# Moving ten of a sample's 32 expert dot-product steps from the output projection to the last dense blocks, in quarters of 512 columns

## The chip, the cores and the metric

The kernel runs on one core of one Trainium2 chip. The metric is device time in microseconds (us), the median of the runs shown. The engines are PE (matrix multiply), DVE (vector), ACT (scalar), POOL (GpSimd, which also issues the gathers) and SP (which here only issues transfers). Each engine executes its own queue strictly in order, and engines wait for one another through semaphores.

## The reference

One decoder layer over 256 prompt tokens and 32 sample tokens (8 sequences of 4): an input projection, an RWKV group and an attention group, one output projection, a layer norm, and then a mixture of 16384 single-row experts. The part that matters here is that last one:

```python
q = (xt @ wq).reshape(n, P_HEADS, 2, P_DKEY // 2)
...
expert = jnp.take_along_axis(cand_e, tpos, axis=-1)
gate = jax.nn.softmax(tv, axis=-1).astype(x.dtype)
...
h = jax.nn.gelu(jnp.einsum('cd,chkd->chk', xb, u_tab[eb]), approximate=False)
return jnp.einsum('chk,chkd->cd', gb * h, v_tab[eb])
```

Every token has 8 heads with 16 chosen experts each, so 128 dot products of its 2048-wide row with rows of `u_tab`. All arrays are float32.

## The kernel before

**Prompt tokens.** The 256 prompt tokens are two tiles of 128 partitions. Their dot products are split by columns. Columns 0 to 895 (`UG`) are done by gathering: for each tile and each of 128 expert slots, `gather` (L453, POOL) fetches one 896-wide row for each partition into a buffer of the ring `rows` (`NRW` = 5 buffers), and one DVE instruction (L1825) multiplies it with the token's row and sums it. There are 256 such dots. The other nine groups of 128 columns (`NDB`) are done densely: for each of 128 blocks `dense(i1)` loads a 576 KB tile `ur` on SP (L1896, `NUR` = 5 buffers), runs 18 matmul instructions on PE (L1899) into one of five PSUM banks `ph`, and copies the result with ACT (L1900) to `AW`. The loop over `i1` spreads the dots that are left evenly over the 128 blocks. In its first 80 blocks DVE also chooses the experts of the second prompt tile (`choose_parts`), and at `i1 == 80` it computes that tile's gates (`gates(1)`, L1454 to L1458, with an exponential on ACT). `table(0)` (L1836 to L1841) follows at block 90.

**The sample.** The 32 sample tokens take all 128 partitions: four groups of heads by 32 tokens, with 32 slots each. So there are 32 *steps*, and each step is a 2048-wide dot product for each partition. `sample_dots` does a step in two halves of 1024 columns: a gather of 512 KB from `uh2` (the table seen as half rows; `GI[2]` and `IG` hold the indices of the first and second halves), and a DVE instruction (L1586) whose sum goes to one column of `hd`. `hd` is a view of a small tile, `shT`, that is no longer needed. The 32 steps run in two places:

- Steps 0 to 13 (`NSD` = 14) at the end of `sample_chain`, in the ring `cw` (`NCW` = 5). The first stands in the attention's weave; the rest are woven with the second half of the output projection: `weave((chain, NSD), (out_part(8, YN), 16, 400))`. The last number gives `out_part` a higher priority in the scheduler.
- Steps 14 to 31, called `late`, in the ring `sr`: six (`NLD`) around the first layer norm, then two for each head of the query projection, all done before the dense blocks.

`sample_formed` then adds the two halves (L1591), applies the Gelu on ACT and multiplies by the gates. Its result is first needed in the stage after the dense blocks (`weigh`).

**The output projection.** `out_part(8, YN)` is 16 pieces of work. A piece loads 512 KB of `w_out` (L1682), makes a rounded copy `wh` on ACT (L1684) and the remainder `wl` on DVE, every fourth on POOL (L1685), each with two buffers, and runs 12 matmuls of 512 columns (L1690). After every four pieces DVE adds the two sums into `x` (L1698) and takes statistics of it (L1699). The layer norm follows.

**What sets the order.** A scheduler with a timeline simulation orders each engine's queue when the kernel is built: by program order as priority, unless something is not ready or its ring has no free buffer. `issue_after` holds instructions behind a named one. After the dense blocks, `pick` (L1933) is the first work of the stage `weigh`.

Of the kernel before, what the change touches and what calls it, by code (L numbers as in the profile page):

```python
# [10 lines left out]
F32 = mybir.dt.float32  # L11
F32R = mybir.dt.float32r
I32 = mybir.dt.int32
U32 = mybir.dt.uint32
AF = mybir.ActivationFunctionType
OP = mybir.AluOpType
AX = mybir.AxisListType
PSUM = bass.MemoryType.PSUM
P = 128

D = 2048
NT = 288
NPR = 256
# [9 lines left out]
WS = 100  # L33
CPOOL = 0
NSO = 4
NSD = 14
NLD = 6
PRI = 200
WB = 4
# [12 lines left out]
NCB = 10  # L52
# [96 lines left out]
def hybrid_decode_step(ctx: ExitStack, tc: tile.TileContext, a, outs, dbg=None):  # L149
# [203 lines left out]
            gp.dma_start(shA[26 * b:26 * b + 26, hf, :],  # L353
                         a["state_shift"][0, 4 * hf + b, 0, :3328].rearrange("(c p) -> c p", p=P))
    shT = cp([P, 2, 4, 26], "shT")
    hd = shT.rearrange("p h b c -> p (h b c)")[:, :64].rearrange("p (q s) -> p q s", q=2)
    def split_x(pb, k_, t_):
        sc.copy(XH0[:, k_, t_], pb)
        ve.tensor_tensor(XL0[:, k_, t_], pb, XH0[:, k_, t_].bitcast(F32), OP.subtract)
# [1052 lines left out]

    def choose_parts(h, pool, S, TV):

        HV, HI, HF = (pool([P, 2, 16], nm, ty) for nm, ty in (("HVb", F32), ("HIb", U32), ("HFb", F32)))
        for c in range(2):
            top16(S[:, c, :], HV[:, c, :], HI[:, c, :])
            yield 1
        for c in range(2):
            ve.tensor_scalar(HF[:, c], HI[:, c], 1.0 if c else 1.0 * P, 0.0, op0=OP.mult, op1=OP.add)  # L1420
        CV, CE = (pool([P, NCAND], nm) for nm in ("CVb", "CEb"))
        for dst, src in ((CV, HV), (CE, HF)):
            o = 0
            for i0, ni, w in CAND:
                ve.tensor_tensor(dst[:, o:o + ni * w].rearrange("p (i j) -> p i j", i=ni),
                                 src[:, 0, i0:i0 + ni, None].to_broadcast([P, ni, w]),
                                 src[:, 1, None, :w].to_broadcast([P, ni, w]), OP.add)
                o += ni * w
        yield 1
        TI, TF = (pool([P, 16], nm, ty) for nm, ty in (("TIb", U32), ("TFb", F32)))  # L1430
        top16(CV, TV[:, h, :], TI)
        ve.tensor_copy(TF, TI)
        yield 1
        hit = rp([P, UG], "rows", bufs=NRW)[:, :16 * NCAND].rearrange("p (a b) -> p a b", a=16)
        ve.tensor_tensor(hit, iota[:, None, :NCAND].to_broadcast([P, 16, NCAND]),
                         TF[:, :, None].to_broadcast([P, 16, NCAND]), OP.is_equal)
        ve.tensor_tensor(hit, hit, CE[:, None, :].to_broadcast([P, 16, NCAND]), OP.mult)
        yield 1
        EF = pool([P, 16], "EFb")
        ve.tensor_reduce(EF, hit, AX.X, OP.add)  # L1440
        sc.copy(GI[1][:, 16 * h:16 * h + 16], EF)
        yield 1
# [44 lines left out]

    w_out, w_q = a["w_out"][0], a["peer_wq"][0]
    utab, vtab = a["peer_u"][0], a["peer_v"][0]
    uh2 = utab.rearrange("n (q c) -> (n q) c", q=2)  # L1490
    iota = C0("iota")

# [87 lines left out]
    def sample_dots(ring, x4, n0, n1):  # L1580

        for s_ in range(n0, n1):
            for q in range(2):
                r_, x_, h_ = ring(), x4[:, 1024 * q:1024 * q + 1024], hd[:, q, s_:s_ + 1]
                gather(r_, uh2, (IG if q else GI[2])[:, s_:s_ + 1])
                ve.scalar_tensor_tensor(r_, r_, 1.0, x_, op0=OP.mult, op1=OP.mult, accum_out=h_)  # L1586
            yield 1

    def sample_formed():

        ve.tensor_tensor(hd[:, 0], hd[:, 0], hd[:, 1], OP.add)  # L1591
        sc.activation(hd[:, 0], hd[:, 0], AF.Gelu)
        ve.tensor_tensor(GE[2], hd[:, 0], GE[2], OP.mult)

# [175 lines left out]
    sx4 = sq_([P, D], "sx4")  # L1770
    for g in range(4):
        sy.dma_start(sx4[32 * g:32 * g + 32, :], X1D[NPR:NT, :])
    late = sample_dots(lambda: sq_([P, 1024], "sr", bufs=5), sx4, NSD, 32)
    with tc.issue_after(normed.ins):
        for _ in take(late, NLD):
            pass
# [53 lines left out]
    def table(t):  # L1830

        pb = bank("pb")
        for q, (op_, v_) in enumerate(((OP.logical_shift_right, 7), (OP.bitwise_and, 127))):
            ii = up([P, P], "ii", I32, bufs=2)
            iff = ii.bitcast(F32)
            ve.tensor_scalar(ii, GI[t], v_, None, op0=op_)  # L1836
            ve.tensor_copy(iff, ii)
            pe.transpose(pb[:, 128 * q:128 * q + 128], iff, ident)
        pe.transpose(pb[:, 256:384], GE[t], ident)
        pe.transpose(pb[:, 384:], HD[t], ident)  # L1840
        sc.copy(TB[:, :, P * t:P * t + P], pb.rearrange("p (a b) -> p a b", a=4))  # L1841
# [34 lines left out]
    with tc.issue_after(chosen.ins), tc.issue_after(last_.ins):  # L1876
        for _ in late:
            pass
        sample_formed()
    sq_.close()  # L1880
    kw_.close()
    for q in range(0, NDB, 3):
# [20 lines left out]
    for i1 in range(P):  # L1903
        mm, end = dense(i1)
        n_ = early + -(-(2 * P - early) * (i1 + 1) // P)
        dot(n_ - got[1])
        with tc.issue_after(last_dot[0].ins):
            for _ in take(later, 6 * (i1 + 1) // NCB - 6 * i1 // NCB):
                pass
            if i1 == 8 * NCB:  # L1910
                for _ in later:
                    pass
                gates(1, up, TV[1])
        if i1 == 8 * NCB + 10:
            with tc.issue_after(mm.ins), tc.issue_after(end.ins):
                table(0)
# [276 lines left out]
```

## Time and profile before

| | |
|---|---|
| median of 3 runs | 2458.02 us (2453.15 to 2464.91) |
| the profiled execution | 2450.29 us, of which 2448.5 us is the span |
| PE, DVE, ACT, POOL busy | 92%, 72%, 34%, 54% of the span |
| moved by the DMA engines | 684.07 MB, 279 GB/s on average |
| second half of the output projection, first matmul to last | 995.33 to 1059.42 us |
| dense blocks on PE, first matmul to last | 1202.3 to 1700 us |
| last dot of the prompt | ends at 1702.2 us |

The table's places are in us from the start of the span. Busy time is an average over stages with different limits, so what matters is which wait ends last in each of the two stages that the change touches: the output projection at about 1000 us, and the last third of the dense blocks, from about 1520 to 1700 us.

### The profile page before, as it was taken

The numbers are of one execution on the slowest core, as the hardware profiler recorded it, in microseconds if no ns is written. First come the engines' busy times: TensorE is split into PE (matmuls) and PEld (weight loads), VectorE is DVE, ScalarE is ACT, GpSimd is POOL, SyncE is SP. The second block draws the span as 40 slices with busy tenths as digits, with TensorE's granted clock in tenths as the row PEclk, the third lists the DMA queues.
The fourth block names the chain that finished last, engine by engine and source line by source line (L and its number), as shares of the span: only waits on it lengthen the run. The fifth ranks groups of instructions, "written<-read, shape, count | busy, mean of one in ns | idle before, by whom it ended". The sixth has DMA issues, their size and how long they took to land.

```text
span 2448.5 us, 42558 instructions
## 1 busy us (share of the span) xinstructions
PE 2255.8 (92%) x15628; PEld 1888.4 (77%) x15628; DVE 1762.0 (72%) x4049; ACT 823.4 (34%) x1601; POOL 1332.6 (54%) x1347
## 2 busy tenths in 40 slices
PE   7988999897988998679999999999999899999996
PEld 7877889894645565558888888887777788887885
DVE  4788766555563355687877777556777899998888
ACT  4433222223432334221111111111777544444343
POOL 5687522324355011666766556565443688886772
PEclk9989999998896799789999999999999999999998
DMA  7777885448578784979999999999664799999994
GB/s 219 215 232 233 257 236 172 131 135 250 200 248 250 249 274 172 317 253 348 317 367 377 391 371 387 345 395 345 186 188 142 284 362 360 358 367 356 345 360 183
DMA packets 327600, 684.07 MB, mean 279 GB/s; under 512 B 82270, under 2 KB 200992, under 8 KB 326464
## 3 DMA queue, kind: packets, MB, share of 16 engines
q1 hardware_dynamic: 246176, 342.58, 42.2%
q0 software_dynamic: 81216, 338.78, 38.6%
q8 instruction: 123, 2.02, 0.3%
q14 instruction: 85, 0.70, 0.1%
HBM read 665.69 MB, written 23.88 MB: 282 GB/s over the span
## 4 chain that ended last, share of the span: by engine, by line
PE 29%; DMA 9%; DVE 8%; issue 7%; POOL 4%; ACT 1%; POOLq 0%; DVEq 0%; SPq 0%; ACTq 0%
PE pb L2107 20%; DMA rows<-in_peer_u_g,gi 8%; POOL rows L453 4%; PE px L1945 3%; DVE rows L1825 2%; PE pa L1978 2%; PE pj L1855 2%; PE pt L1937 1%; PE fs L1997 1%; DVE sr L1586 1%; DVE vl L2100 1%; DMA wraw<-in_peer_wq 0%; ACT vh L2099 0%; PE pa L1690 0%; DVE cw L1586 0%
## 5 line engine op out<-in xcount | busy, mean ns | idle before, releaser
L1899 PE MATMUL ph<-Xfd,ur 128*128 128x256 f32 x2304 | 497.6, 379 | 0.0
L1899 PEld LDWEIGHTS ph<-Xfd,ur 128*128 128x128 f32 x2304 | 437.6, 190 | 59.4
L453 POOL DMA_INDIRECT rq<-in_peer_v_g,gi x256 | 382.2, 1493 | 145.8 <-DVE fP L2080 85.6
L453 POOL DMA_INDIRECT rows<-in_peer_u_g,gi x256 | 313.3, 1224 | 189.3 <-DVE rows L1825 119.0
L1825 DVE SCALAR_TENSOR_TENSOR rows<-rows,x1a 128x896 f32<-128x896 f32 x256 | 278.8, 1097 | 136.2 <-DMA rows<-in_peer_u_g,gi 135.5
L422 PE MATMUL pj<-XH,wl 128*128 128x288 f32 (+1 forms) x752 | 233.5, 311 | 15.8 <-DVE wl L417 9.1
L422 PE MATMUL pj<-XH,wh 128*128 128x288 f32 (+1 forms) x752 | 232.1, 309 | 14.6 <-DVE ss L752 6.0
L422 PE MATMUL pj<-XL,wh 128*128 128x288 f32 (+1 forms) x752 | 228.0, 303 | 0.0
L2080 DVE SCALAR_TENSOR_TENSOR fP<-rq,ge,fP 128x640 f32<-128x640 f32 x254 | 223.7, 881 | 2.5
L2107 PE MATMUL pb<-vl,ah 128*128 128x512 f32 (+1 forms) x768 | 205.9, 376 | 0.8
L2107 PE MATMUL pb<-vh,al 128*128 128x512 f32 (+1 forms) x768 | 205.0, 375 | 0.0
L1900 ACT COPY AW<-ph 128x256 f32<-128x256 f32 x128 | 76.6, 612 | 370.5 <-PE ph L1899 362.7
L2107 PE MATMUL pb<-vh,ah 128*128 128x512 f32 (+1 forms) x768 | 185.6, 376 | 13.4 <-ACT vh L2099 10.9
L415 ACT CAST wh<-wraw 128x512 fp32r<-128x512 f32 (+1 forms) x188 | 115.1, 616 | 240.3 <-PE pj L422 191.1
L2107 PEld LDWEIGHTS pb<-vh,ah 128*128 128x128 f32 x768 | 144.1, 194 | 35.5 <-ACT vh L2099 13.9
L422 PEld LDWEIGHTS pj<-XH,wl 128*128 128x128 f32 (+1 forms) x752 | 145.8, 194 | 26.8 <-DVE wl L417 12.4
L476 DVE SCALAR_TENSOR_TENSOR CA<-co,wbc,CA 128x256 f32<-128x256 f32 x248 | 131.5, 568 | 46.5 <-DMA co<-in_cache_cmp_kv,gidx 46.5
L422 PEld LDWEIGHTS pj<-XH,wh 128*128 128x128 f32 (+1 forms) x752 | 146.1, 194 | 21.0 <-ACT wh L415 6.7
L2107 PEld LDWEIGHTS pb<-vl,ah 128*128 128x128 f32 x768 | 144.1, 194 | 22.7 <-DVE vl L2100 3.8
L2107 PEld LDWEIGHTS pb<-vh,al 128*128 128x128 f32 x768 | 144.5, 194 | 19.3
L422 PEld LDWEIGHTS pj<-XL,wh 128*128 128x128 f32 (+1 forms) x752 | 146.4, 195 | 1.5 <-issue 1.2
L417 DVE TENSOR_TENSOR wl<-wraw,wh 128x512 fp32r<-128x512 f32 (+1 forms) x141 | 100.8, 722 | 49.0 <-ACT wh L415 48.7
(871 smaller groups left out, 4335.6 us busy)
## 6 DMA issues: line engine op xcount, KB each, us to landing
ur<-in_peer_u_t SPq DMA_DIRECT2D x128, 576.0 KB
wraw<-in_w_in SPq DMA_DIRECT2D x152, 256.0 KB
cw<-in_w_out SPq DMA_DIRECT2D x32, 512.0 KB
wraw<-in_w_out SPq DMA_DIRECT2D x32, 512.0 KB
wraw<-in_peer_wq SPq DMA_DIRECT2D x32, 512.0 KB
cw<-in_peer_wq SPq DMA_DIRECT2D x32, 512.0 KB
wraw<-in_w_in SPq DMA_DIRECT2D x64, 128.0 KB
co<-in_state_win_kv SPq DMA_DIRECT2D x16, 512.0 KB
```

The source lines that it names most:

```text
L415: sc.copy(wh[:, :, :n], w[:, :, :n])
L417: i_ = en.tensor_tensor(wl[:, :, :n], w[:, :, :n], wh[:, :, :n].bitcast(F32), OP.subtract)
L422: last[2] = pe.matmul(pb[:n, :nt], wi[:, k, :n], xi[(o + k) // 8][:, (o + k) % 8, :nt], start=(o + k == 0 and wi is wh and xi is xh), stop ...
L453: gp.indirect_dma_start(out=dst, out_offset=None, in_=rows_, in_offset=bass.IndirectOffsetOnAxis(ap=ix, axis=0))
L476: ve.scalar_tensor_tensor(d_, x_, w_, d_, op0=OP.mult, op1=OP.add)
L1825: i_ = ve.scalar_tensor_tensor(r_, r_, 1.0, X1a[t], op0=OP.mult, op1=OP.mult, accum_out=h_)
L1855: pe.matmul(pb[:, :NPR], w[:, k, :], XT[:, o + k, :], start=(o + k == 0), stop=(o + k == 15))
L1899: mm = pe.matmul(ph[:, :NPR], w[:, e, :], Xfd[:, e, :], start=(e == 0), stop=(e == NDB - 1))
L1900: return mm, sc.copy(AW[:, i1 // 64, :, i1 % 64], ph[:, :NPR])
L1945: pin(pe.matmul(px[:, 128 * e:128 * e + 128].rearrange("p (c j) -> p c j", c=2), oT[:, e, :], AW[:, :, 4 * u + e, :], start=True, stop=True))
L2080: ve.scalar_tensor_tensor(fP[t], r_, w_, fP[t], op0=OP.mult, op1=OP.add)
L2107: pe.matmul(acc[3 * t + q][:, :n_], wi[:, P * t:P * t + P], xi[:, 512 * q:512 * q + n_], start=(k == 0 and wi is ah and xi is vh), stop=(k ...
```

## The change

Of the sample's 32 steps, only four (0 to 3) stay at the end of `sample_chain`; `late` now holds steps 4 to 21, again 18 steps; and steps 22 to 31 (`NSU` = 10) go into the loop over the dense blocks, one each at blocks 82, 86, ..., 118. There a step is four quarters of 512 columns, each with a gather of 256 KB from `uq4` into a buffer of the ring `rows`, shared with the prompt's dots, and a DVE instruction with a sum of its own. For them the sample's rows are loaded again on SP (four transfers, at block 80) into the place of the scores `S1`, and four small DVE instructions compute the indices after the gates. `sample_formed` moves behind the last of these steps. Besides, `choose_parts` now uses the tiles that `choose` used before it instead of its own, and `table` has a third buffer `ii`.

```diff
-NSD = 14
+NSD = 4
+NSU = 10
...
-    hd = shT.rearrange("p h b c -> p (h b c)")[:, :64].rearrange("p (q s) -> p q s", q=2)
+    sh_ = shT.rearrange("p h b c -> p (h b c)")
+    hd = sh_[:, :64].rearrange("p (q s) -> p q s", q=2)
+    hx, ix = (t_[:, 64 + 4 * NSU * n:64 + 4 * NSU * (n + 1)].rearrange("p (s q) -> p s q", q=4)
+              for n, t_ in enumerate((sh_, sh_.bitcast(I32))))
...
-        HV, HI, HF = (pool([P, 2, 16], nm, ty) for nm, ty in (("HVb", F32), ("HIb", U32), ("HFb", F32)))
+        HV, HI, HF = (pool([P, 2, 16], nm, ty) for nm, ty in (("HV", F32), ("HI", U32), ("HF", F32)))
...
+    uq4 = utab.rearrange("n (q c) -> (n q) c", q=4)
...
-        ve.tensor_tensor(hd[:, 0], hd[:, 0], hd[:, 1], OP.add)
+        ve.tensor_tensor(hd[:, 0, :32 - NSU], hd[:, 0, :32 - NSU], hd[:, 1, :32 - NSU], OP.add)
+        ve.tensor_reduce(hd[:, 0, 32 - NSU:], hx, AX.X, OP.add)
         sc.activation(hd[:, 0], hd[:, 0], AF.Gelu)
...
-    late = sample_dots(lambda: sq_([P, 1024], "sr", bufs=5), sx4, NSD, 32)
+    late = sample_dots(lambda: sq_([P, 1024], "sr", bufs=5), sx4, NSD, 32 - NSU)
...
-            ii = up([P, P], "ii", I32, bufs=2)
+            ii = up([P, P], "ii", I32, bufs=3)
...
-        sample_formed()
...
                 gates(1, up, TV[1])
+                for q in range(4):
+                    ve.tensor_scalar(ix[:, :, q], GI[2][:, 32 - NSU:], 2.0, float(q), op0=OP.mult, op1=OP.add)
+        if i1 == 8 * NCB:
+            x4 = dp([P, 8, 2 * P], "S1").rearrange("p a b -> p (a b)")
+            for g in range(4):
+                sy.dma_start(x4[32 * g:32 * g + 32, :], X1D[NPR:NT, :])
+        if i1 > 8 * NCB and i1 % 4 == 2 and i1 // 4 - 2 * NCB < NSU:
+            k = i1 // 4 - 2 * NCB
+            with tc.issue_after(last_dot[0].ins):
+                for q in range(4):
+                    r_ = rp([P, UG], "rows", bufs=NRW)[:, :512]
+                    gather(r_, uq4, ix[:, k, q:q + 1])
+                    ve.scalar_tensor_tensor(r_, r_, 1.0, x4[:, 512 * q:512 * q + 512], op0=OP.mult, op1=OP.mult,
+                                            accum_out=hx[:, k, q:q + 1])
+                if k == NSU - 1:
+                    sample_formed()
```

More of the change, by code (lines that the diff above doesn't have):

```diff
@@ L1420, in choose_parts @@
             ve.tensor_scalar(HF[:, c], HI[:, c], 1.0 if c else 1.0 * P, 0.0, op0=OP.mult, op1=OP.add)
-        CV, CE = (pool([P, NCAND], nm) for nm in ("CVb", "CEb"))
+        CV, CE = (pool([P, NCAND], nm) for nm in ("CV", "CE"))
         for dst, src in ((CV, HV), (CE, HF)):
@@ L1429, in choose_parts @@
         yield 1
-        TI, TF = (pool([P, 16], nm, ty) for nm, ty in (("TIb", U32), ("TFb", F32)))
+        TI, TF = (pool([P, 16], nm, ty) for nm, ty in (("TI", U32), ("TF", F32)))
         top16(CV, TV[:, h, :], TI)
@@ L1438, in choose_parts @@
         yield 1
-        EF = pool([P, 16], "EFb")
+        EF = pool([P, 16], "EF", bufs=2)
         ve.tensor_reduce(EF, hit, AX.X, OP.add)
```

## Prediction

> **What bounds the kernel now.** I read the page's head and its chain of waits first, to see which stages the end hangs on; then the busy time in stretches of 10 us in the two stages touched; then, in each, who waited for whom, the groups, and each engine's order of time.
>
> The page:
>
> ```profile
> span 2448.5 us, 42558 instructions
> PE 29%; DMA 9%; DVE 8%; issue 7%; POOL 4%; ACT 1%; POOLq 0%; DVEq 0%; SPq 0%; ACTq 0%
> PE pb L2107 20%; DMA rows<-in_peer_u_g,gi 8%; POOL rows L453 4%; PE px L1945 3%; DVE rows L1825 2%; PE pa L1978 2%; PE pj L1855 2%; PE pt L1937 1%; PE fs L1997 1%; DVE sr L1586 1%; DVE vl L2100 1%; DMA wraw<-in_peer_wq 0%; ACT vh L2099 0%; PE pa L1690 0%; DVE cw L1586 0%
> ```
>
> The prompt's gathers (rows: transfer, POOL, DVE) are the second largest part of the chain, after the last stage's matmuls. The steps that leave the projection (cw L1586) round to 0%, but the shares only add to some 58%: the chain is lost before the projection is over, so its stage has to be read from its own waits.
>
> The end of the dense blocks. Three stretches of 10 us (busy PE, PEld, DVE, ACT, POOL, then granted clock, DMA share, GB/s), the third for comparison with the first two:
>
> ```profile
> 1540.00:1550.00 10.00, 10.00 (x48) 8.79 (x48) 0.00 (x0) 2.94 (x5) 1.65 (x2) 1.00 0.90 332
> 1550.00:1560.00 10.00, 10.00 (x50) 8.82 (x49) 6.69 (x18) 2.15 (x5) 4.20 (x4) 1.00 0.71 242
> 1650.00:1660.00 10.00, 10.00 (x48) 8.81 (x47) 6.13 (x11) 1.49 (x3) 5.73 (x6) 1.00 1.02 409
> ```
>
> The transfers of 1570 to 1690 us and the gathers issued in them:
>
> ```profile
> DMA packets 9505, 47.43 MB, mean 395 GB/s; under 512 B 1519, under 2 KB 1519, under 8 KB 9497
> rows<-in_peer_u_g,gi POOLq DMA_INDIRECT x64, 7.6
> ```
>
> The groups of 1551 to 1703 us (busy, mean ns, idle time before and what ended it), then the gathers and the dots of that window by tile, with the landing times:
>
> ```profile
> L453 POOL DMA_INDIRECT rows<-in_peer_u_g,gi x77 | 95.8, 1244 | 59.5 <-DVE rows L1825 45.6 <-issue 12.7 <-ACT AW L1900 1.2
> L1825 DVE SCALAR_TENSOR_TENSOR rows<-rows,x1a 128x896 f32<-128x896 f32 x82 | 89.0, 1093 | 58.1 <-DMA rows<-in_peer_u_g,gi 58.0
> ```
>
> ```profile
> L453 POOL DMA_INDIRECT rows<-in_peer_u_g,gi x77: 951/957/1872, 1552.6 to 1695.5; - x77
> L1825 DVE DVE_READ_ACCUMULATOR rows<-rows,x1a x82: 77/83/85, 1552.3 to 1702.2; 128x1 f32 x82
> DMA to landing us min/median/max: 5.0/7.5/8.3
> ```
>
> The tile `ur` (first and last start), and DVE in order of time:
>
> ```profile
> L1899 PE MATMUL ph<-Xfd,ur x2304: 379/379/382, 1202.3 to 1699.8; 128*128 128x256 f32 x192
> L1896 SPq DMA_DIRECT2D ur<-in_peer_u_t x128: 327/328/1104, 1180.0 to 1680.8; - x128
> ```
>
> ```profile
> 1550.50 0.29 DVE L1456 TENSOR_REDUCE sm<-ge 128x8 f32<-128x128 f32 x1 [11.69 <-ACT ge L1455]
> 1556.11 0.36 DVE L1836 TENSOR_SCALAR ii<-gi 128x128 int32<-128x128 int32 x2 [2.74 <-PE pb L1838]
> ```
>
> PE is full and never waits for `ur`: (1699.8-1202.3)/128 = 3.89 us a block. The dots end at 1702.2, 2.4 us behind PE, so two things end this stage together. The dots are not held by an engine: DVE is idle 58 us of the 151 from 1551 to 1702, always for a transfer, and POOL waits 45.6 us for a buffer that DVE frees. They are held by transfers: from 1570 to 1690 (the 47.43 MB row) the DMA engines move 395 GB/s at a share of about 1.0, and 64 gathers are issued, one per 120/64 = 1.88 us. The only slack is 1540 to 1560, where DVE stood 11.69 us for the gates' exponential and then 2.74 us for `table(0)`.
>
> The projection, in two stretches, then its waits and groups of 975 to 1062 us:
>
> ```profile
> 1010.00:1020.00 10.00, 10.00 (x34) 7.92 (x34) 4.97 (x8) 2.65 (x3) 4.34 (x4) 0.73 1.03 402
> 1050.00:1060.00 10.00, 8.43 (x36) 6.28 (x35) 9.97 (x13) 1.90 (x2) 3.14 (x1) 1.00 0.74 264
> ```
>
> ```profile
> PE pa L1690 <- DVE wl L1685: 11.5, 6, 5.9
> PE pb L727 <- DVE O L721: 5.6, 1, 5.6
> PE pa L1690 <- POOL wl L1685: 1.7, 2, 1.5
> ```
>
> ```profile
> L1586 DVE SCALAR_TENSOR_TENSOR cw<-cw,x 128x1024 f32<-128x1024 f32 x28 | 35.8, 1298 | 13.1 <-DMA cw<-in_peer_u,gi 6.8 <-DMA cw<-in_peer_u,ig 6.3
> L453 POOL DMA_INDIRECT cw<-in_peer_u,ig x14 | 19.5, 1394 | 10.1 <-DVE cw L1586 5.9 <-issue 2.3 <-DVE su L715 1.0
> ```
>
> DVE, PE and POOL in order of time (start, duration, and in brackets the idle time before), and the transfers of 980 to 1004 us:
>
> ```profile
> 1003.65 1.23 DVE L1586 SCALAR_TENSOR_TENSOR cw<-cw,x 128x1024 f32<-128x1024 f32 x1 [4.90 <-DMA cw<-in_peer_u,gi]
> 1007.91 1.22 DVE L1685 TENSOR_TENSOR wl<-wraw,wh 128x1024 fp32r<-128x1024 f32 x1
> ```
>
> ```profile
> 995.33 0.78 PE L1690 MATMUL pa<-wh,YH 128*128 128x512 f32 x1
> 1009.19 0.79 PE L1690 MATMUL pa<-wl,YH 128*128 128x512 f32 x1 [5.86 <-DVE wl L1685]
> 1009.78 0.63 PE L1690 MATMUL pa<-wh,YH 128*128 128x512 f32 x1
> 1010.21 0.63 PE L1690 MATMUL pa<-wh,YL 128*128 128x512 f32 x1
> 1016.05 0.39 PE L1690 MATMUL pa<-wh,YH 128*128 128x512 f32 x1
> 1016.28 0.39 PE L1690 MATMUL pa<-wh,YL 128*128 128x512 f32 x1
> 1059.03 0.39 PE L1690 MATMUL pa<-wl,YH 128*128 128x512 f32 x1
> ```
>
> ```profile
> 1040.52 1.97 POOL L453 DMA_INDIRECT cw<-in_peer_u,ig  x1 [0.30 <-ACT wh L1684]
> 1042.51 2.54 POOL L1685 TENSOR_TENSOR wl<-wraw,wh 128x1024 fp32r<-128x1024 f32 x1
> ```
>
> ```profile
> DMA packets 1743, 6.73 MB, mean 280 GB/s; under 512 B 227, under 2 KB 227, under 8 KB 1617
> ```
>
> Here the steps do stand in the way. At 1003.65 DVE had stood 4.90 us for a gathered half; the remainder `wl` stood behind that dot until 1007.91, and PE waited 5.86 us for it. It then ran slowly: 0.43 us from matmul to matmul (1009.78 to 1010.21) against 0.23 at 1016, with the granted clock at 0.73 in that stretch. On POOL the remainder of 1042.51 came right behind a gather.
>
> **The change, part by part.** All of it is against the profiled execution, 2450.29 us, which lies 7.7 us below the median of 2458.02.
>
> *Taken from the projection:* ten steps, each two gathers (20 x 1.39 = 28 us of POOL) and two dots (20 x 1.298 = 26.0 us of DVE), 10.5 MB. On the path lie only PE's waits. Ahead of `wl` on DVE and POOL the dots and gathers go, so I take both waits as gone, 11.5 + 1.7 = 13.2 us, and with the long one the slow stretch after it, some 15 matmuls x (0.43-0.23) = 3.0 us: **-16.2 us**. What is late next is PE itself. Low end: only the longest wait and its slow stretch go, 5.9 + 3.0 = 9 us. High end: the 26.0 us of DVE time. PE has 192 matmuls in this half; at 0.23 us they need 44 of the 64.1 us from 995.33 to the end at 1059.4, so 26 would take 20 from PE's waits and the 5.6 us before its first matmul besides. I don't count those 5.6: the four steps that stay are the ones on DVE then.
>
> *Added to the dense blocks:* ten steps of four gathers of 128x512x4 = 262144 B, 10.49 MB, and the sample's rows once more on SP, 128x2048x4 = 1.05 MB: 11.53 MB in all, from block 82 (1202.3 + 82 x 3.89 = 1521 us) on. DMA is full there and PE takes its weights first, so the extra ends up behind 1690 us. At 395 GB/s it takes 29.2 us; at 280, the row nearest to gathers without the weights, 41.2 us. The leftover is a mix of dots and quarters, part of it still beside weights, so I take the middle, 35.2; the ends stay for the range.
>
> *The same gathers as engine time:* POOL has 77 + 40 gathers from 1552 us on; at 1.244 + 0.30 us between two of them they need 181 of 151 us, +30; without the slow ones (0.96 us), nothing. So POOL stays just under DMA. DVE: a dot of 512 columns is at most the 1.09 us of 896 columns and by its width 1.093 x 512/896 = 0.62 us; with 0.08 to read the sum, 40 x 0.70 = 28 us, in 58 us of idle time: nothing. Were it not covered it would cost those 28.
>
> *Small edits.* The third `ii` may remove the 2.74 us wait: -2.7 us; zero at worst. The four index instructions, 10 columns each: two of 128 columns take 0.36 us together (1556.11), so under 0.2 us each, nothing. The new load stands on SP ahead of `ur` loads and waits for the last read of `S1`; the last `ur` load is issued at 1680.8 and its block starts some 15 us later, so a wait of up to 15 us is covered, above it PE stops for the rest. `sample_formed` puts a Gelu into ACT's queue that waits for the tenth step, and the copies of later blocks stand behind it; five banks x 3.89 = 19 us cover that, and PE's last ten blocks would still end before a stream that is 30 us late. The tile names shared by `choose_parts` cost nothing: their former users are past.
>
> *Sum:* -16.2 + 35.2 - 2.7 = **+16.3 us**: the profiled execution would take 2466.6, the median 2474.
>
> The Trainium skill, page "DMA: Bandwidth & Descriptors", section "Where 436 GB/s comes from", says that transfers between HBM and SBUF are bound by about 358 GB/s for a core. By it the 11.53 MB would cost an estimated 32.2 us instead of 29.2; this trace moves 395 GB/s for 120 us, so the row decides.
>
> **The rivals.** A change of 0.5%, 12.3 us, is about what a measurement of this kernel can tell from none.
>
> *The ring sets the pace (slower by about 35).* The forecast has quarters pass at the DMA's rate. But they share five buffers with the dots. A buffer is taken by a quarter for at least the fastest landing seen, 5.0 us, a dot of 0.70 and a gap of 0.30, 6.0 us; or 7.0 if the gather's own 0.96 isn't in the landing time. Divided by five that is 1.2 to 1.4 us a quarter, 48 to 56 us for 40; less 2.7 and 16.2, +29 to +37. For it: POOL waits for buffers 45.6 us already. Against it: under a full DMA the landing time is itself a queue, and half the bytes land sooner. The Trainium skill's page "DMA: Bandwidth & Descriptors", section "Anatomy of one DMA — SWDGE (gpsimd) path", gives each transfer issued from GpSimd a fixed 2.0 us beside its bytes over 436 GB/s, an estimated 2.6 us for a quarter against 3.2 for a half, so by it four quarters hold their buffers longer than two halves. The median landing of 7.5 us here is far above either, so this trace shows mostly queueing.
>
> *It comes out even.* The slack of 1540 to 1560 (77 and 167 GB/s short of 409, so 2.4 MB) is filled by the first steps, and the rest goes at 409: (11.53-2.4)/0.409 = 22.3 us, less 2.7, against 16.2: +3. For it: DMA has been seen at 409. Against it: the first steps come after the gates in program order, and POOL stood still in that slack for want of buffers.
>
> *Faster.* One mechanism: all the DVE time taken out is on the projection's path, -26.0. With the tail just described, +19.6, that gives -6, and down to -18 if the first steps also fill DVE's 11.69 us wait for the gates. It decides where the projection's gain exceeds the tail's loss, so above about 20 us. For it: DVE is busy 9.97 of 10 us at the stage's end. Against it: PE's 44 us, above.
>
> *The change doesn't do what it says:* the quarters could wait until all dots are through, as both need ring buffers. But the dots behind a step have lower priority, so I only see them mixed; the bytes, and so the time, would be the same.
>
> **How the numbers follow.** The forecast 0.50, its own range +6 to +29 (tail 29.2 to 41.2 less 2.7, gain 9 to 20); of that, 0.14 lies under 12.3 us. The ring 0.17. Even 0.15. Faster 0.18, of which 0.10 beyond -12.3: I count there too what the scheduler may place better elsewhere. So faster 0.10, same 0.14 + 0.15 + 0.08 = 0.37, slower 0.36 + 0.17 = 0.53. The time is the forecast's, 2474; the range runs from -11 (2447) to +36 (2494), where the ring's prices end, and leaves out about 0.1 on each side.
>
> **What would show it.** Right: PE's waits for `wl` in the projection drop from 13.2 to a few us and its matmuls need about 48 us; the last dot falls some 30 us behind the last dense matmul, with DMA share 1.0 up to PE's end and lower rates after it; the transfers stay near 395 GB/s. Wrong: POOL or DVE filled in the tail with DMA below 0.9 (ring or engine); the last dot within 10 us of PE's end (even or faster); `wl` still waited for, now behind ACT; PE idle among the dense blocks, behind the new SP load or the Gelu.

## The result and the profile after

The changed kernel takes 2483.88 us (median of 6 runs, 2479.72 to 2499.6) against 2455.59 us (6 runs, 2443.19 to 2464.91) before: a ratio of 1.0128 (95% interval 1.0089 to 1.0168), slower by 1.3%. Forecast were 2474 (2447 to 2494), likeliest slower. The profiled execution took 2480.57 us with a span of 2478.8, so the spans differ by 2478.8-2448.5 = 30.3 us. All below is read against that.

The page of the changed kernel, chain of waits by engine and by line:

```profile
PE 71%; DMA 8%; DVE 8%; issue 6%; POOL 5%; ACT 2%; SPq 1%; DVEq 0%; POOLq 0%; ACTq 0%
PE pb L2128 18%; PE ph L1904 14%; PE pj L426 8%; PE pj L1861 4%; PE pa L1696 4%; PE px L1966 3%; PE p L1083 2%; PE pa L1999 2%; POOL rows L457 2%; DMA rows<-in_peer_u_g,gi 2%; PE pt L1958 2%; PE ss L1532 1%; PE fs L2018 1%; DVE CA L480 1%;
```

Before, PE held 29% of the chain and the chain could not be followed further back. Now it runs back through the projection (pa L1696) and the dense matmuls (ph L1904), and then through the gathers and dots of the tail: neither side of the stage covers the other any more.

**The projection.** The last product of its matmuls, first and last start, before and then after:

```profile
L1690 PE MATMUL pa<-wl,YH x128: 387/393/794, 808.2 to 1059.0; 128*128 128x512 f32 x128
```

```profile
L1696 PE MATMUL pa<-wl,YH x128: 387/389/793, 804.0 to 1036.0; 128*128 128x512 f32 x128
```

The two halves of the projection, with the attention between them, take 232.0 us instead of 250.8, which is 18.8 less. This is more than the chance of one execution: the other kernel below with the old projection (e8) takes 251.1, and the eleven with the new one 224.8 to 232.7. PE's waits of 975 to 1040 us (its weight loads, which see a late tile first), and two stretches (columns as in the prediction):

```profile
PEld pb L731 <- DVE O L725: 5.4, 1, 5.4
...
PEld pa L1696 <- POOL wl L1691: 0.6, 3, 0.2
PEld pa L1696 <- DVE wl L1691: 0.3, 1, 0.3
```

```profile
1000.00:1010.00 10.00, 10.00 (x45) 8.27 (x45) 5.98 (x7) 4.22 (x4) 1.31 (x2) 1.00 0.93 338
1020.00:1030.00 10.00, 10.00 (x45) 8.16 (x45) 5.74 (x7) 4.02 (x4) 2.39 (x1) 1.00 0.59 188
```

In both stretches PE is full and its clock is 1.00. Its matmuls' waits for `wl` (13.2 us before) are gone from the list, and its weight loads wait 0.9 us for it (16.6 before). The wait ahead of the half, for `O`, stayed.

**The end of the dense blocks.** The dense matmuls and the dots (count, ns of the shortest, median and longest, first and last start):

```profile
L1904 PE MATMUL ph<-Xfd,ur x2304: 379/379/454, 1178.0 to 1676.3; 128*128 128x256 f32 x192
```

```profile
L1831 DVE DVE_READ_ACCUMULATOR rows<-rows,x1a x256: 75/83/88, 1124.9 to 1731.8; 128x1 f32 x128
L1931 DVE DVE_READ_ACCUMULATOR rows<-rows,S x40: 76/82/84, 1543.2 to 1714.1; 128x1 f32 x40
```

From 1480 to 1760 us, who waited for whom:

```profile
PEld pb L1846 <- DVE rows L1831: 55.2, 1, 55.2
...
DVE ii L1842 <- ACT gi L1445: 19.4, 1, 19.4
...
DVE ii L1842 <- PE pb L1844: 1.4, 1, 1.4
```

PE ends at 1676.7 and then waits 55.2 us for the last dot, at 1731.8; before, the dots ended 2.0 us behind PE (1702.2 against 1700.2). So the 30.3 us are made up like this (after less before): up to the projection -4.2, where nothing was changed; from its first matmul to the first dense one 374.6-394.7 = -20.1; the dense blocks +0.8; from PE's end to the last dot +53.1; from there to the end 747.0-746.3 = +0.7.

Stretches beside PE and behind its end, and the transfers of the 120 us before that end and of the tail:

```profile
1600.00:1610.00 10.00, 10.00 (x48) 8.81 (x47) 4.62 (x13) 1.21 (x2) 7.08 (x7) 1.00 0.96 338
1680.00:1690.00 10.00, 0.00 (x0) 0.00 (x0) 6.58 (x12) 0.00 (x0) 7.47 (x6) 0.51 0.95 332
1690.00:1700.00 10.00, 0.00 (x0) 0.00 (x0) 5.85 (x13) 0.00 (x0) 7.74 (x7) 0.50 0.74 225
1700.00:1710.00 10.00, 0.00 (x0) 0.00 (x0) 7.01 (x16) 0.00 (x0) 8.06 (x7) 0.50 0.86 283
```

```profile
DMA packets 9602, 43.24 MB, mean 360 GB/s; under 512 B 1573, under 2 KB 1573, under 8 KB 9594
...
DMA packets 2911, 14.92 MB, mean 271 GB/s; under 512 B 565, under 2 KB 565, under 8 KB 2910
```

The rate falls to 360 GB/s already beside PE, where 395 had been forecast to last, and to 271 behind it, with POOL's row rising to 7.5 to 8.1 of 10 us. POOL in order of time in the tail (start, duration, idle time before):

```profile
1688.19 1.75 POOL L457 DMA_INDIRECT rows<-in_peer_u,shT  x1 [0.30 <-DVE rows L1831]
1690.24 0.96 POOL L457 DMA_INDIRECT rows<-in_peer_u,shT  x1 [0.30 <-issue]
1691.50 0.96 POOL L457 DMA_INDIRECT rows<-in_peer_u,shT  x1 [0.30 <-DVE rows L1831]
1692.77 1.37 POOL L457 DMA_INDIRECT rows<-in_peer_u,shT  x1 [0.30 <-issue]
1694.44 1.03 POOL L457 DMA_INDIRECT rows<-in_peer_u_g,gi  x1 [0.31 <-issue]
```

A quarter takes POOL as long as a gather of 896 columns (1.13 and 1.09 us in the mean from 1540 to 1735 us), and the next follows 0.30 us later. How many dots and quarters passed, by the groups of DVE in the 120 us before PE's end and in the 30 us after it:

```profile
L1831 DVE SCALAR_TENSOR_TENSOR rows<-rows,x1a 128x896 f32<-128x896 f32 x45 | 49.3, 1097 | 38.4 <-DMA rows<-in_peer_u_g,gi 36.1 <-DVE rows L1831 1.7 <-issue 0.6
L1931 DVE SCALAR_TENSOR_TENSOR rows<-rows,S 128x512 f32<-128x512 f32 x27 | 18.6, 697 | 15.0 <-DMA rows<-in_peer_u,shT 14.0 <-issue 0.5 <-DVE rows L1931 0.5
...
L1831 DVE SCALAR_TENSOR_TENSOR rows<-rows,x1a 128x896 f32<-128x896 f32 x13 | 14.2, 1094 | 9.7 <-DMA rows<-in_peer_u_g,gi 9.6
L1931 DVE SCALAR_TENSOR_TENSOR rows<-rows,S 128x512 f32<-128x512 f32 x6 | 4.2, 692 | 3.4 <-DMA rows<-in_peer_u,shT 3.4
```

Beside PE 45 + 27 = 72 tiles pass in 120 us, one per 1.67 us (e9 below, without quarters, passes 66 tiles of full size there, one per 1.82). So a quarter, 0.57 of a full tile's bytes, buys nearly nothing. Behind PE 19 tiles come in the first 30 us, one per 1.58 us, and up to the last dot 36 (26 dots and 10 quarters) in 55.1 us, one per 1.53.

### The profile page after: what moved, and what is told of

Read it like the earlier page. It is cut to its first block, busy times and chain, and to the rows that moved or that the text cites. A ratio compares the mean times of both kernels' runs of the same rounds, so it can differ in the third digit from the quotient of the medians.

```text
span 2478.8 us, 42670 instructions
## 1 busy us (share of the span) xinstructions
PE 2251.8 (91%) x15628; PEld 1885.5 (76%) x15628; DVE 1764.5 (71%) x4094; ACT 821.5 (33%) x1599; POOL 1339.2 (54%) x1367
## 4 chain that ended last, share of the span: by engine, by line
PE 71%; DMA 8%; DVE 8%; issue 6%; POOL 5%; ACT 2%; SPq 1%; DVEq 0%; POOLq 0%; ACTq 0%
PE pb L2128 18%; PE ph L1904 14%; PE pj L426 8%; PE pj L1861 4%; PE pa L1696 4%; PE px L1966 3%; PE p L1083 2%; PE pa L1999 2%; POOL rows L457 2%; DMA rows<-in_peer_u_g,gi 2%; PE pt L1958 2%; PE ss L1532 1%; PE fs L2018 1%; DVE CA L480 1%; PE sa L924 1%
## 5 line engine op out<-in xcount | busy, mean ns | idle before, releaser
L1904 PE MATMUL ph<-Xfd,ur 128*128 128x256 f32 x2304 | 497.8, 379 | 0.6 <-DMA ur<-in_peer_u_t 0.6
L1904 PEld LDWEIGHTS ph<-Xfd,ur 128*128 128x128 f32 x2304 | 437.5, 190 | 60.3 <-issue 0.9
L457 POOL DMA_INDIRECT rows<-in_peer_u_g,gi x256 | 303.7, 1186 | 187.5 <-DVE rows L1831 100.6
```

The source lines that it names most:

```text
L457: gp.indirect_dma_start(out=dst, out_offset=None, in_=rows_, in_offset=bass.IndirectOffsetOnAxis(ap=ix, axis=0))
L1904: mm = pe.matmul(ph[:, :NPR], w[:, e, :], Xfd[:, e, :], start=(e == 0), stop=(e == NDB - 1))
```

## The experiments

All are compared with runs of the kernel before on the same chip, whose medians were 2450.5 to 2452.7 us. "Behind PE" is the last dot less the end of the dense matmuls (last start + 0.4); it is read from one profiled execution of each kernel.

**e1, no quarters.**

```diff
-                for q in range(4):
-                    r_ = rp([P, UG], "rows", bufs=NRW)[:, :512]
...
+                if k == 0:
+                    ve.memset(hx, 0.0)
```

> The changed kernel without its ten moved steps at all: their 40 gathers and 40 dots are left out (their sums are set to zero), so this is the projection's gain alone. All theories agree on the place: the dense blocks start some 20 us earlier than in the kernel before, and the last dot ends within 5 us of the last dense matmul again. In time: my forecast's term of 16.2 us gives about 2439 us beside a before of 2455; if the 24 us by which the dense blocks start earlier in the changed kernel are all the change's doing, about 2432; if part of them is chance, 2445.

2455.11 us, ratio 1.0008 (0.9968 to 1.0048): my expectation missed, the gain did not come through. The last dot was 18.1 us behind PE with no quarter in the stream. DVE's waits from 1480 us on:

```profile
DVE rows L1831 <- DMA rows<-in_peer_u_g,gi: 65.3, 76, 3.3
DVE ge L1599 <- ACT shT L1598: 20.3, 1, 20.3
DVE ii L1842 <- ACT gi L1445: 11.5, 1, 11.5
```

`sample_formed` still stood at the tenth step's place, among the last dense blocks. Its Gelu (L1598) went into ACT's queue behind the copies of the blocks and DVE, next in order, waited 20.3 us for it. The dots that are left after block 118 can't make that up.

**e2, half the bytes in as many gathers.**

```diff
-    uq4 = utab.rearrange("n (q c) -> (n q) c", q=4)
+    uq4 = utab.rearrange("n (q c) -> (n q) c", q=8)
...
-                    r_ = rp([P, UG], "rows", bufs=NRW)[:, :512]
+                    r_ = rp([P, UG], "rows", bufs=NRW)[:, :256]
```

The indices and the dots follow (256 columns each); the other half of each quarter is left out.

> The changed kernel with 256 columns in each of the 40 moved gathers and dots instead of 512 (half of the ten steps' sums is left out): as many gathers, half the bytes (5.24 MB less). In the changed kernel the 40 quarters lengthen the dots' stream by some 51 us. If that is bytes, it falls to 26 us and the time to about 2459; if it is a turn of the ring or an issue on POOL, the same for every gather, it stays at 51 and the time at 2484; a mix, a fixed 0.5 us and the rest by bytes, gives 36 us and about 2469.

2482.36 us, ratio 1.0139 (1.0079 to 1.0199); 50.5 us behind PE instead of 55.1: the number expected if every gather costs the same. 5.2 MB fewer moved nothing that the times can tell. Bytes are not what the tail costs. Nor is it the DMA engines' time for a row whatever its bytes: their share falls from 0.96 to 0.92 in the 120 us before PE's end, and from 0.83 to 0.78 behind it, at the same pace of the stream.

**e3, half the gathers with 0.87 of the bytes:** 20 of 896 columns, and dots to match; 256 columns of each step are left out.

```diff
-                for q in range(4):
-                    r_ = rp([P, UG], "rows", bufs=NRW)[:, :512]
-                    gather(r_, uq4, ix[:, k, q:q + 1])
+                for q in range(2):
+                    r_ = rp([P, UG], "rows", bufs=NRW)
+                    gather(r_, a["peer_u_g"], ix[:, k, q:q + 1])
```

> The changed kernel with two gathers of 896 columns for each of the ten moved steps instead of four of 512 (the last 256 columns of these steps are left out; the gathered rows come from the prompt's table): half as many gathers, 9.18 MB instead of 10.49. If the 51 us are bytes, 45 us and about 2478; if they are a fixed turn for each gather, 26 us and about 2459; the mix (0.5 us a gather and the rest by bytes), 37 us and about 2470.

2470.3 us, ratio 1.0109 (1.0047 to 1.017); 34.2 us behind PE. That is near the mix of the expectation (37 us, 2470), not the half that a fixed turn alone would give (26 us, 2459). The interval overlaps that of the changed kernel, so the weight lies on the 34.2 us. With e2 it shows that the number of gathers counts, more than the bytes. Size counts a little beside PE: 67 tiles, all of full size, pass in the 120 us before its end, against 72 in the changed kernel.

**e4, a ring of six,** paid for with one buffer of `ur` (four instead of five).

```diff
-NUR = 5
+NUR = 4
...
+NRR = 6
...
-                    r_ = rp([P, UG], "rows", bufs=NRW)[:, :512]
+                    r_ = rp([P, UG], "rows", bufs=NRR)[:, :512]
```

> The changed kernel with six buffers in the ring that dots and quarters share, instead of five; the tile ur gets four instead of five to make room, whose cover falls from 15 to about 12 us. If the ring sets the pace, the stream from the gates to the last dot (206 us) passes up to a sixth faster, down to 172 us, and the time falls to about 2450. If the DMA's bytes set it while PE runs, and POOL's issue after that, nothing changes: 2484 within 5 us, and the landing times get longer by a fifth.

2461.54 us, ratio 1.0047 (1.0022 to 1.0072). The dense matmuls and the dots:

```profile
L1905 PE MATMUL ph<-Xfd,ur x2304: 378/379/796, 1183.1 to 1693.0; 128*128 128x256 f32 x192
```

```profile
L1832 DVE DVE_READ_ACCUMULATOR rows<-rows,x1a x256: 75/82/85, 1130.0 to 1719.5; 128x1 f32 x128
```

26.2 us behind PE, though PE itself took 510.3 us instead of 498.7. From the first dense matmul to the last dot it is 536.5 us instead of 553.8: a sixth buffer gives 17 us back, with all 40 quarters and their bytes in place. The time lies between the two that were expected, 2450 and 2484. The ring is one of the limits.

**e5, DVE's wait for ACT taken out of the stream.** In the tail's rows DVE waits 19.4 us for ACT's copy of the second tile's indices (`GI[1]`). ACT in order of time there:

```profile
1504.52 0.61 ACT L1905 COPY AW<-ph 128x256 f32<-128x256 f32 x1 [3.28 <-PE ph L1904]
...
1524.75 0.60 ACT L1905 COPY AW<-ph 128x256 f32<-128x256 f32 x1 [3.29 <-PE ph L1904]
1525.15 0.21 ACT L1445 CAST gi<-EF 128x16 int32<-128x16 f32 x1
```

The value to copy was there at about 1506; the copy of 0.21 us stood behind block copies that each wait 3.3 us for PE. The Trainium skill, page "Perfetto Trace Analysis", section "Tensor Engine Instruction (MATMUL, LD_WEIGHTS)", says in a remark that ACT, DVE and GPSIMD work strictly first in, first out; the rows agree.

```diff
-        sc.copy(GI[1][:, 16 * h:16 * h + 16], EF)
+        ve.tensor_copy(GI[1][:, 16 * h:16 * h + 16], EF)
...
-                gates(1, up, TV[1])
...
         if s_ == 20:
+            gates(1, up, TV[1])
             table(1)
```

> The changed kernel with one wait of DVE taken away: the copy of the second tile's indices (GI[1], the one that table(1)'s first operation waits for) is done by DVE instead of by ACT, and gates(1), whose exponential is ACT's, moves to the last stage ahead of table(1). Theory (the dots' stream on DVE and POOL ends the dense blocks, so what stops DVE there for 19.4 us costs that much): the last dot comes 15 to 20 us earlier, some 37 us behind the last dense matmul instead of 55, and the time falls to 2462-2470. Rival (each gather has a fixed turn and POOL alone counts; the wait is made up by the ring's five full buffers): less than 5 us, 2479-2484.

2483.78 us, ratio 1.0143 (1.0098 to 1.0188); 54.0 us behind PE. Inconclusive: the scheduler put the gates back among the dense blocks, and DVE waited 11.5 us for their exponential and 8.6 for `table(1)`'s transposes, 20.1 in all. The wait changed its name only.

**e6, the ten steps in the last stage:** 20 halves of 1024 columns beside the first 30 groups of `weigh`; the Gelu of the other 22 steps ahead of the dense blocks.

```diff
+        if s_ % 3 == 2 and s_ < 30:
+            rest_dot(s_ // 3)
+        if s_ == 34:
+            sample_rest()
```

> The ten steps leave the projection as in the changed kernel, but go to the last stage (beside its first 30 groups) as 20 halves of 1024 columns, none to the dense blocks. Theory (what the projection gives, some 20 us, is lost again wherever DVE's wait for ACT stands in the dots' stream): the dense blocks start some 20 us earlier than before, the dots still end some 15 us behind PE, and the last stage takes 0 to 10 us more for 20 gathers in it: 2448-2462, even with before. Rival (the dense blocks' end follows PE, 498 us behind their start): 2432-2445.

2497.35 us, ratio 1.0207 (1.0157 to 1.0257): both numbers missed. Yet the first part came out as the rival had it: the dense blocks began at 1181.3 and the last dot fell 0.1 us behind PE, at 1679.3, 22.9 us earlier than before. Then the last stages took 2495.0-1679.3 = 815.7 us instead of 746.3, 69 more. A stretch of that stage before, and the same of e6:

```profile
1760.00:1780.00 20.00, 19.92 (x163) 16.17 (x160) 16.34 (x71) 14.95 (x42) 9.52 (x8) 1.00 0.60 192
```

```profile
1760.00:1780.00 20.00, 12.79 (x87) 10.62 (x87) 11.65 (x43) 7.60 (x20) 7.44 (x7) 0.76 0.54 164
```

No engine is full there in e6. The stage's order is written out; as I read it, a wait of DVE for a gathered half holds up what it does next for PE. In that stretch PE's granted clock is 0.76 besides.

**e7, e6 and e5 together.**

```diff
+        if s_ % 3 == 2 and s_ < 30:
+            rest_dot(s_ // 3)
...
+            gates(1, up, TV[1])
             table(1)
```

> Both: the ten steps in the last stage, and DVE's wait for ACT taken away as in e5. Theory: the dots' stream now ends within 5 us of PE, the projection's 20 us come through, less 0 to 10 us in the last stage: 2433-2448, faster than before by about 0.3 to 0.9 per cent. Rival (the dots' stream is too long for the dense blocks even without the wait): as e6, 2448-2462.

2495.14 us, ratio 1.018 (1.0134 to 1.0226): missed as e6, in the same place (68 us in the last stages).

**e8, e5's edit on the kernel before.**

> The kernel before with the same wait taken away and nothing else (14 steps beside the projection). Theory: its dots end 2.4 us behind PE, so taking away their 14 us of waits frees only those: 2449-2456, the same as before. Rival (the wait costs its full length there too): 2438-2444.

2451.02 us, ratio 0.999 (0.9962 to 1.0018), as expected, but with little weight: as in e5 DVE's waits for ACT and PE were still there (16.1 us, 14.4 before).

**e9, no steps and no late Gelu:** e6 without the 20 halves, their sums set to zero.

```diff
-        if s_ % 3 == 2 and s_ < 30:
-            rest_dot(s_ // 3)
+        if s_ == 2:
+            ve.memset(hd[:, :, 32 - NSU:], 0.0)
+            ve.memset(hx[:, :, 0], 0.0)
```

> The ten steps are left out altogether (their sums set to zero) and the Gelu of the others stands ahead of the dense blocks, not among them, so that neither gathers nor a late Gelu are added to the dots' stream; ACT's copy of the indices stays. Against e1 it lacks only the late Gelu, against e6 the 20 gathers of the last stage. Theory (the projection gives some 20 us, and the dots' stream, about as long as PE's 498 us, lets them through when nothing is added to it): the last dot within 3 us of the last dense matmul, the last stages as before (747 us behind the last dot), 2428-2437. Rival (the stall on the index copy alone keeps the dots behind PE): as e1, 2448-2460.

2425.85 us, ratio 0.9878 (0.9826 to 0.9929). The dense matmuls, the dots, and DVE's waits from 1480 to 1700 us:

```profile
L1915 PE MATMUL ph<-Xfd,ur x2304: 379/379/483, 1186.0 to 1685.2; 128*128 128x256 f32 x192
```

```profile
L1841 DVE DVE_READ_ACCUMULATOR rows<-rows,x1a x256: 74/81/86, 1133.0 to 1684.3; 128x1 f32 x128
```

```profile
DVE rows L1841 <- DMA rows<-in_peer_u_g,gi: 64.1, 81, 3.6
DVE ii L1852 <- ACT gi L1445: 13.7, 1, 13.7
```

The group of its dots in the 120 us before PE's end, 66 tiles:

```profile
L1841 DVE SCALAR_TENSOR_TENSOR rows<-rows,x1a 128x896 f32<-128x896 f32 x66 | 72.2, 1096 | 46.2 <-DMA rows<-in_peer_u_g,gi 46.1
```

The last dot comes 1.2 us before PE's end: what the projection gives, goes through to the end of the kernel when nothing is added to the dots' stream. It goes through in spite of 13.7 us of DVE standing for the index copy at about block 80, so a wait of that size, this early, costs nothing. Against e1, which has the late Gelu, the span is 25.5 us shorter; e1 also has the index instructions and the second load of the sample's rows among the dense blocks, which e9 has not.

**e10, two gathers to a buffer:** 40 gathers of 448 columns, each pair in one buffer with one dot of 896; bytes, dots and turns of the ring as in e3.

```diff
+                    for c in range(2):
+                        gather(r_[:, UG // 2 * c:UG // 2 * c + UG // 2], ug2, ix[:, k, c:c + 1])
```

> The changed kernel with 40 gathers of 448 columns, two of them to one buffer of the ring, and one dot of 896 columns for the pair: bytes, dots and turns of the ring as in e3 (20 gathers of 896), the number of gathers as in the changed kernel; 256 columns of each step are left out as there. Theory (the ring's five buffers set the pace, a fixed turn for each buffer): the last dot some 34 us behind PE as in e3, 2466-2474. Rival (POOL's time for each gather, 0.96 us and more plus 0.3 between two, sets it): some 50-55 us behind PE, 2478-2486.

2490.63 us, ratio 1.0175 (1.0127 to 1.0223); 56.3 us behind PE against e3's 34.2: the rival's numbers. The quarters' group on POOL from 1540 to 1735 us:

```profile
L457 POOL DMA_INDIRECT rows<-in_peer_u_g,shT x36 | 51.4, 1427 | 12.6 <-issue 9.1 <-DVE rows L1832 3.1 <-DMA rows<-in_peer_u_g,shT 0.3
```

The quarters' gathers hardly wait for buffers here (3.1 us) and take POOL 1.43 us each, with 0.3 between two. Behind PE POOL is busy 40.9 of the 56.3 us, 7.9 more go in such gaps and 5.2 in waits for buffers. So I read POOL as the limit; but a buffer here is also bound for two gathers, so a turn of the ring is longer than in e3, and the run does not separate the two.

**e11, e6 with the gathers three groups ahead of their dots.**

```diff
+        if s_ % 2 and 5 <= s_ < 45:
+            rest_fetch((s_ - 5) // 2)
+        if s_ % 2 == 0 and 8 <= s_ < 48:
+            rest_dot((s_ - 8) // 2)
```

> As e6, the ten steps in the last stage as 20 halves of 1024 columns, but each is gathered three groups ahead of its dot, from group 5 on, one half every other group up to 47, and the rows of the second table for these steps follow after that. Theory (e6 lost its 66 us there because DVE, in its written order, stood for each transfer; DVE's own work for the steps, 28 us, finds 4.4 idle us in each 20 of a stage that PE bounds): the last stage takes 5 to 20 us more than before, less the 20 of the projection: 2435-2455. Rival (DVE's added time is on the path there in full, or the ring of five is too short for both tables): 30 us and more, 2460-2480.

2484.12 us, ratio 1.0126 (1.0086 to 1.0165): missed. Its last stages are no shorter than e6's (2505.1-1690.5 = 814.6 us). Waits of 1700 to 1900 us:

```profile
POOL rows L457 <- PE fs L2035: 68.9, 17, 6.7
...
POOL rows L457 <- DVE xj L1972: 43.2, 9, 15.0
...
DVE rows L2022 <- DMA rows<-in_peer_u,ig: 25.0, 10, 4.3
DVE rows L2022 <- DMA rows<-in_peer_u,gi: 17.0, 8, 8.9
```

DVE still waits 42.0 us for halves that come late. POOL's wait for PE, which frees the buffers of the second table's rows, is no cause by itself: the kernel before has 78.4 us of it in the same window. New are the 43.2 us that POOL waits for DVE (at `xj`, its products of PE's sums there); the kernel before has none of these. How these waits make up the 68 us is open.

**e12, the quarters by plain loads on SP:** same bytes, row lengths, buffers and dots, 40 gathers fewer on POOL.

```diff
-                    gather(r_, uq4, ix[:, k, q:q + 1])
+                    sy.dma_start(r_, utab[P * k:P * k + P, 512 * q:512 * q + 512])
```

> The changed kernel with the 40 quarters brought by plain loads on SP's queue (128 rows of 512 columns from fixed places of the same table, into the same ring of five, with the same dots) in place of POOL's gathers: bytes, row lengths, turns of the ring and DVE's work as in the changed kernel, but 40 gathers fewer on POOL. The rows are not those that the indices name, so the sums of the ten steps are other numbers. Theory (while PE runs the DMA engines pass about one gather per 1.7 us whatever its size, so some 35 are left behind PE, and each then costs POOL 1.4 to 1.5 us): of those left, only the dots' own gathers cost POOL's time, the last dot comes some 25 to 35 us behind PE instead of 55, 2455-2466. Rival (the ring's turns or the transfers set it, whoever issues them): 50-55 us behind PE, 2478-2486. If SP's waits for the ring's buffers hold up PE's weights, the dense blocks take more than 499 us, and the time is to be read by the last dot alone.

2490.7 us, ratio 1.0163 (1.0099 to 1.0227); 62.9 us behind PE. The dense blocks took 502.7 us, more than the 499 of the condition, so the last dot alone counts: it ends at 1738.5, 565.6 us behind the first dense matmul, against 553.8 in the changed kernel. The theory that POOL's time alone sets the pace fell. POOL in order of time in the tail:

```profile
1699.90 1.16 POOL L457 DMA_INDIRECT rows<-in_peer_u_g,gi  x1 [6.96 <-DVE rows L1831]
1701.37 0.95 POOL L457 DMA_INDIRECT rows<-in_peer_u_g,gi  x1 [0.30 <-issue]
```

Now POOL stands 7 us at a time for buffers that the four quarters of a step hold, and then issues seven gathers in a row. The ring is the limit, at the same pace. Part of this may be the edit's own doing: from 1699.55 us DVE takes the four quarters of a step without a wait, so they had landed before and held their buffers behind the dots ahead of them.

**What they say together.** Two limits lie side by side, as I read it. One is the ring: five buffers, each bound from its gather's issue to the end of its dot. The other is POOL's issue of a gather. Freed of one, the stream runs into the other at nearly the same rate:

| kernel | tiles added | behind PE | per tile | limit, as I read it |
|---|---|---|---|---|
| e9 | 0 | -1.2 us | | |
| after | 40 gathers of 256 KB | 55.1 us | 1.4 us | both |
| e2 | 40 gathers of 128 KB | 50.5 us | 1.3 us | both |
| e3 | 20 gathers of 448 KB | 34.2 us | 1.7 us | both |
| e10 | 40 gathers of 224 KB in 20 buffers | 56.3 us | 1.4 us | POOL |
| e12 | 40 plain loads of 256 KB | 62.9 us | 1.6 us | ring |

The time per tile is the column before it over the number of gathers or loads. It holds whatever more DVE waited for ACT and PE in that run. These waits were 18.2 us in e9, where they cost nothing, 11.4 in e10, 12.1 in e2, 22.0 after, 24.6 in e3 and 26.2 in e12; if each us above 18.2 costs one, e3 comes to 1.4 and e12 to 1.4. How much they cost was not separated, since e5 only renamed them. Nor were POOL and the ring relieved together.

Counted in DVE's groups between PE's end and the last dot, 36 tiles stand behind PE in the changed kernel, 34 in e2, 22 in e3 and 42 in e12. That is 1.53, 1.49, 1.55 and 1.50 us a tile, whatever its size and whoever brings it. With six buffers (e4) it is 19 tiles at 1.38 us, and POOL's waits for buffers in that stretch fall from 6.6 to 0.9 us; with two gathers to a tile (e10) it is 31 at 1.82. So the count of tiles behind PE is shown, and that the sixth buffer helps. Which of the two limits holds at each place is argued.

No version was found that beats the kernel before and does all its work: a step costs some 5.5 us (55.1/10) among the last dense blocks and 6.9 in the last stage, and about 2 beside the projection.

## Why the prediction was right or wrong

**The direction** (slower) was right, and the range held the time. The likeliest case was too low by 10 us (28.3 us between the medians, 16.3 forecast); 30.3 us between the profiled executions is the figure of the rival called the ring, +29 to +37. That the time stayed within the range was partly luck. The tail alone, 53.1 us, lies outside the 29.2 to 41.2 that I gave it; a larger gain in the projection, and the 4.2 us ahead of it where nothing was changed, made up for part. My own sign for "ring or engine" came true: POOL near full in the tail, with the DMA share at 0.83 in the mean behind PE.

**Taken from the projection, -16.2 us:** right in mechanism, near in size. 18.8 us went between its matmuls and 20.1 up to the dense blocks, at the top of the stated 9 to 20. `wl` is no longer waited for, the slow stretch is gone, the `O` wait that I did not count stayed, and the second half needs 46 us (990.6 to 1036.4) against the 48 forecast. The faster rival, with all 26 us of DVE time on the path, fell for the reason given against it: PE's own matmuls came next.

**Added to the dense blocks, +35.2 us:** this is the step that failed, measured at 53.1. I priced the leftover by its bytes; by e2 the bytes cost at most 55.1-50.5 = 4.6 us for half of them, and DVE waited 9.9 us less for ACT and PE in that run. What is left behind PE is tiles, by count. Beside PE the stream passed 72 tiles in 120 us where 66 full ones passed, so of the 40 it took up only some 6. That leaves about 34, and 36 were counted behind PE, at 1.53 us each: 55.1 us. Nor did the rate of 395 GB/s last: beside PE it is 360 with quarters, 334 in e2, at DMA shares of 0.96 and 0.92. Whether 395 was the ring's rate or the DMA's for full tiles, no run separates. The Trainium skill, page "DMA: Bandwidth & Descriptors", section "Anatomy of one DMA — SWDGE (gpsimd) path", says that a transfer has a fixed cost of about 2.0 us beside its bytes over 436 GB/s. The runs agree in kind only, since theirs is the spacing in a stream and not the time of one transfer: from 128 to 448 KB a gather cost 1.3 to 1.7 us.

**The same gathers as engine time.** I had the row (1.244 + 0.30 us, +30 us for POOL), and set it aside because most gathers take 0.96. In the tail POOL was busy 7.5 to 8.1 of 10 us with the 0.30 gaps on top, that is, nearly full. At 1.4 us a quarter, the price of the ring's rival, the 40 come to 56 us, the right size.

**The ring as a rival, 1.2 to 1.4 us a quarter:** right in size (1.4). My reason against it, that under a full DMA the landing time is a queue that shrinks with the bytes, is what the runs refute: with half the bytes the pace stayed (e2). It is perhaps not the only limit: with half the buffers' turns, but as many gathers, the stream came no earlier (e10).

**The third `ii`, -2.7 us:** wrong in sign, and small. DVE's wait for the table's transposes fell from 2.74 to 1.4 us, but `table(1)`'s first instruction, which I take to be free to move up by the third buffer, stood 19.4 us for ACT. No run took the third buffer out alone. In all DVE waited 22.0 us for ACT and PE there instead of 14.4; the 7.6 more cost at most that.

**The rest.** PE did not stand behind the new load (0.6 us once), DVE's quarters were covered, and the late Gelu cost nothing here, since it comes behind the last quarter when PE is through. But my sentence on it looked only at copies behind the Gelu. The cost lies the other way, a Gelu behind the copies, with DVE waiting: 20.3 us in e1.

## What to carry to other kernels

In this kernel a stream of gathers through a small ring was paid by the tile. So before cutting a transfer into pieces that fit a buffer, count the pieces and price each at the ring's turn and at the issuing engine's time, whichever is longer, not at its bytes. A stage in which two streams end together may have no room for more, however idle its engines look. A short operation that another engine waits for should not go through a queue of copies that wait for PE: it waits for them all.

## What the runs showed of the hardware that I had not expected

- A gather of 128 rows takes POOL between 0.95 and 1.97 us, and 1.43 in the mean where two pieces went to one buffer (e10); what makes it slow was not found.
- Plain loads of 128 rows by 512 columns, which cost POOL nothing, passed through the same ring no faster than gathers (42 tiles behind PE in e12 at 1.50 us each, 36 at 1.53 after).
- While PE stood in the tail its granted clock was 0.50, and the row of e6 shows 0.76 in a stretch in which PE was busy 12.8 of 20 us.
